# Token products that read their weight columns as pairs from the two halves of the row

## The chip, the core and the metric

The kernel runs on one core of a Trainium2 chip. Its time is the device time of one execution in microseconds (us); lower is better. The core has TensorE (PE in the profile; its weight loads are PEld), VectorE (DVE), ScalarE (ACT), GpSimd (POOL) and SyncE (SP, which issues the DMAs here). SBUF is the working memory with 128 partitions; PSUM holds eight banks of 512 float32 for each partition, into which the matmuls write.

## The reference

It is a decoder trunk with two layers over 256 tokens and 2048 channels, in float32. Layer 0 mixes by causal pooling, layer 1 by attention with dilated windows; each is followed by a gated MLP of width 5504 with a short convolution in time. Two products of layer 1 matter here:

```python
v_shared = (h @ shared_w_v).reshape(B_, S, N_HEADS, HEAD_DIM)
...
def conv_ffn(h, w_up, conv_w, conv_b, w_down):
    u = h @ w_up
    ...
    return (jax.nn.silu(gate) * val) @ w_down
...
ff = conv_ffn(h, ffn_w_up[i], ffn_conv_w[i], ffn_conv_b[i], ffn_w_down[i])
h = layer_norm(DEEPNORM_ALPHA * h + ff, ln2_g[i], ln2_b[i])
```

## The kernel before

Each float32 number is split into a high part `h`, rounded to the type fp32r, and a low part `l`, the rest. A product x w is computed as three: high by high, high by low and low by high. A matmul has a stationary operand of 128 x 128, loaded into TensorE's array, and a moving operand whose columns are streamed through it, up to 512 at a time.

The work is a list of **units**. A unit is a block of a weight matrix, mostly 512 x 512: one DMA of 1 MB brings it to `raw` (`do_load`), ScalarE rounds it to `wh` and VectorE subtracts to get `wl` (`do_split`, L76 and L77), and TensorE uses both. `run_units` goes through the list; loads run up to six units ahead and splits up to three. What follows a product is attached to its last unit (`post`) or put off by some units (`later`).

Most products have the channels as rows of the result: the weights are stationary and the 256 tokens are the moving operand (`mm_quad`, called by `group`; L135 streams 512 columns, high and low part of the tokens as two runs of 256; L136 and L138 to L140 stream 256).

Two families of products have the **tokens as rows** (`group_tm`): there 128 tokens are stationary (`xh`, `xl`), and the weights are moving, 512 columns of `wh` or `wl` at a time. For each of the two halves of the tokens (t = 0, 1) and each block k of 128 input channels there are three matmuls, L162 to L164, that accumulate in the bank `ps[t]`, which the profile calls `t`. These families are

- the values of the attention, `shared_w_v`, four groups of four units, one group after each quarter's keys and queries. `v_post` copies the two banks to `vt`, by ScalarE (L657) and VectorE (L659);
- the down projection of layer 1's MLP, `ffn_w_down[1]`: 43 blocks of 128 input channels by four column groups, in four rounds. `tm_post` adds each finished bank to the residual `HT` (`ht` in the profile) on VectorE (L603). In the last round the layer norm follows: the statistics of each column group (L608), then `finish`, and the output is stored. The last column group does its two token halves one after the other (`apart`).

The order of the instructions on each engine is that of the program text, by units; there is no planner. TensorE's banks come from a pool of eight.

## Time and profile before

| what | value |
|---|---|
| median of 3 runs | 2078.8 us (2077.95 to 2078.83) |
| profiled execution | 2079.46 us |
| its span in the profile | 2077.2 us |
| granted TensorE clock in it | 0.997 of full speed |
| busy: TensorE / VectorE / ScalarE | 99% / 68% / 50% |
| HBM read over the span | 380.01 MB, 184 GB/s read and written |

The span is the time from the first to the last instruction that the profile shows; the execution's time is some 2 us more. "Busy" counts the time in which an engine has at least one instruction under way. A group of the profile is read as line, engine, operation, result <- operands, shapes and count, then total busy time in us and mean duration in ns, then the engine's idle time just before these instructions in us and what ended it. In the profile, "PE 128x512" is a matmul with 512 columns. Numbers of an engine in a window stand as busy us with the count of instructions in brackets. The chain that ended last is followed from the last instruction back to whatever released each step.

### The profile page before, as it was taken

Reading aid. Unit: us, or ns where it says so; the run is one execution under the profiler, and the core shown is the slowest. Engines: PE = TensorE matmul, PEld = TensorE weight load, DVE = VectorE, ACT = ScalarE, POOL = GpSimd, SP = SyncE. Lnnn points to the kernel's source line nnn. Section 1 sums busy time; section 2 is a strip of 40 time slices with the busy share of each in tenths; the row PEclk is TensorE's granted clock in tenths of the full one; section 3 lists DMA queues with packets and bytes.
Section 4 is the critical chain, followed back from the end, with each engine's and each line's share of the span. In section 5 each row is a group of like instructions: output and inputs, shape, how many; then the busy total and the mean of one; then the engine's idle time right before and its main releaser. Section 6 shows DMA issues by size and latency. Waiting matters only on the chain.

```text
span 2077.2 us, 28936 instructions
## 1 busy us (share of the span) xinstructions
PE 2062.0 (99%) x12131; PEld 1819.3 (88%) x12131; DVE 1417.2 (68%) x1765; ACT 1029.2 (50%) x1145; POOL 11.4 (1%) x38
## 2 busy tenths in 40 slices
PE   9999999999999999999999999999999999999997
PEld 9998998888888888889888888999888888888886
DVE  6758787756756766788855667787646664665676
ACT  6545665345534535546644444475535543544553
POOL 2000000000000000000000000000000000000000
PEclk9999999999999999999999999999999999999999
DMA  8655465555555555555555555545555555555453
GB/s 261 214 186 195 148 211 175 202 182 186 180 203 183 183 197 178 178 177 167 199 168 178 162 171 175 197 148 202 184 199 185 183 190 195 183 184 192 162 198 137
DMA packets 195298, 383.99 MB, mean 185 GB/s; under 512 B 7022, under 2 KB 15876, under 8 KB 194912
## 3 DMA queue, kind: packets, MB, share of 16 engines
q1 hardware_dynamic: 194240, 381.71, 53.8%
q8 instruction: 95, 1.56, 0.3%
q0 software_dynamic: 928, 0.44, 0.1%
q14 instruction: 35, 0.29, 0.0%
HBM read 380.01 MB, written 2.10 MB: 184 GB/s over the span
## 4 chain that ended last, share of the span: by engine, by line
PE 98%; DVE 1%; DMA 0%; SPq 0%; issue 0%; ACT 0%; DVEq 0%
PE acc L135 44%; PE acc L136 23%; PE t L162 5%; PE t L164 5%; PE t L163 5%; PE acc L139 5%; PE acc L138 5%; PE acc L140 5%; DVE wl L77 0%; PE s L693 0%; PE o L733 0%; DVE ht L633 0%; PE pT L720 0%; DMA xin<-in_x_dram 0%; PE o L734 0%; PE s L692 0%
## 5 line engine op out<-in xcount | busy, mean ns | idle before, releaser
L77 DVE TENSOR_TENSOR wl<-raw,wh 128x2048 fp32r<-128x2048 f32 (+2 forms) x376 | 821.1, 2187 | 514.8 <-ACT wh L76 504.9
L76 ACT CAST wh<-raw 128x2048 fp32r<-128x2048 f32 (+2 forms) x376 | 685.3, 1828 | 594.3 <-PE acc L135 367.9
L135 PE MATMUL acc<-xc,wh 128*128 128x512 f32 x2752 | 969.1, 396 | 0.0
L136 PE MATMUL acc<-xc,wl 128*128 128x256 f32 x2752 | 772.1, 281 | 0.0
L135 PEld LDWEIGHTS acc<-xc,wh 128*128 128x128 f32 x2752 | 519.1, 189 | 122.2
L136 PEld LDWEIGHTS acc<-xc,wl 128*128 128x128 f32 x2752 | 519.0, 189 | 0.2
L135 PE MATMUL acc<-g,wh 128*128 128x512 f32 x688 | 241.9, 396 | 0.0
L136 PE MATMUL acc<-g,wl 128*128 128x256 f32 x688 | 193.0, 280 | 0.0
L135 PEld LDWEIGHTS acc<-g,wh 128*128 128x128 f32 x688 | 129.9, 189 | 30.6
L518 DVE SCALAR_TENSOR_TENSOR c<-u,cv,c 128x256 f32<-128x256 f32 x344 | 141.9, 478 | 0.7
L162 PE MATMUL t<-wh,g 128*128 128x512 f32 x344 | 136.1, 396 | 0.0
L163 PE MATMUL t<-wl,g 128*128 128x512 f32 x344 | 135.5, 394 | 0.0
L164 PE MATMUL t<-wh,g 128*128 128x512 f32 x344 | 135.4, 394 | 0.0
L136 PEld LDWEIGHTS acc<-g,wl 128*128 128x128 f32 x688 | 130.0, 189 | 0.0
L139 PE MATMUL acc<-xp,wh 128*128 128x258 f32 x384 | 109.2, 284 | 0.0
L138 PE MATMUL acc<-xc,wh 128*128 128x256 f32 x384 | 109.2, 284 | 0.0
L138 PE MATMUL acc<-xp,wh 128*128 128x258 f32 x384 | 109.0, 284 | 0.0
L140 PE MATMUL acc<-xc,wl 128*128 128x256 f32 x384 | 108.8, 283 | 0.0
L139 PE MATMUL acc<-xc,wh 128*128 128x256 f32 x384 | 108.7, 283 | 0.0
L140 PE MATMUL acc<-xp,wl 128*128 128x258 f32 x384 | 107.9, 281 | 0.0
L505 ACT COPY ut<-acc 128x256 f32<-128x256 f32 x140 | 51.6, 371 | 96.3 <-PE acc L136 96.1
L135 PE MATMUL acc<-o,wh 128*128 128x512 f32 x256 | 90.4, 396 | 0.0
(182 smaller groups left out, 2310.8 us busy)
## 6 DMA issues: line engine op xcount, KB each, us to landing
raw<-in_ffn_w_up_dram SPq DMA_DIRECT2D x160, 1024.0 KB, 4.9
raw<-in_ffn_w_down_dram SPq DMA_DIRECT2D x80, 1024.0 KB, 5.0
raw<-in_pool_w_out_dram SPq DMA_DIRECT2D x16, 1024.0 KB, 5.1
raw<-in_shared_w_k_dram SPq DMA_DIRECT2D x16, 1024.0 KB, 5.0
raw<-in_attn_w_q_dram SPq DMA_DIRECT2D x16, 1024.0 KB, 5.1
raw<-in_shared_w_v_dram SPq DMA_DIRECT2D x16, 1024.0 KB, 5.0
raw<-in_attn_w_o_dram SPq DMA_DIRECT2D x16, 1024.0 KB, 5.1
raw<-in_pool_w_in_dram SPq DMA_DIRECT2D x12, 1024.0 KB, 5.3
```

What stands on the lines that cost most here:

```text
L76: A.copy(wh[i][:, s], r[:, s])
L77: V.tensor_tensor(wl[i][:, s], r[:, s], wh[i][:, s].bitcast(F32), OP.subtract)
L135: PE.matmul(ps[m], h[:, k, c], q[:, k, :, :T], start=st, stop=False)
L136: PE.matmul(ps[m][:, :T], l[:, k, c], q[:, k, 0, :T], start=False, stop=sp)
L138: PE.matmul(ps[m][:, :n], h[:, k, c], q[:, k, 0, :n], start=st, stop=False)
L139: PE.matmul(ps[m][:, :n], h[:, k, c], q[:, k, 1, :n], start=False, stop=False)
L140: PE.matmul(ps[m][:, :n], l[:, k, c], q[:, k, 0, :n], start=False, stop=sp)
L162: PE.matmul(ps[t], xh, h[:, k, :], start=j == 0 and k == 0, stop=False)
L163: PE.matmul(ps[t], xh, l[:, k, :], start=False, stop=False)
L164: PE.matmul(ps[t], xl, h[:, k, :], start=False, stop=j == len(r0s) - 1 and k == nk - 1)
L505: A.copy(t, ps[m][:, T:])
L518: V.scalar_tensor_tensor(c[:, m, :], u[:, m, i:i + T], cv[:, i, j:j + 1], c[:, m, :], op0=OP.mult, op1=OP.add)
```

## The change

In `group_tm` the moving operand is read through a view, `twine`: columns 0, 256, 1, 257, 2, 258 and so on, so pairs from the two halves of the 512 columns of a row. The matmul writes its 512 results in a row in the bank, in that order. Where the bank is read, `untwine` takes its words 0, 2, 4 ... as the first half and 1, 3, 5 ... as the second, and `halves2` shows the destination as two halves. The values computed and the places where they end up are those of before. It touches the 1416 matmuls with tokens as rows, the additions to `HT` and the copies to `vt`.

```diff
+    def twine(w):
+        return w.rearrange("p (a c) -> p c a", a=2)
+
+    def untwine(ps):
+        return ps.rearrange("p (c a) -> p a c", a=2)
+
+    def halves2(v):
+        return v.rearrange("p (a c) -> p a c", a=2)
+
     def group_tm(w, r0s, c0, ncol, xqs, post, apart=False):
...
             for k in range(nk):
                 xh, xl = q[:, k, 0, s], q[:, k, 1, s]
-                PE.matmul(ps[t], xh, h[:, k, :], start=j == 0 and k == 0, stop=False)
-                PE.matmul(ps[t], xh, l[:, k, :], start=False, stop=False)
-                PE.matmul(ps[t], xl, h[:, k, :], start=False, stop=j == len(r0s) - 1 and k == nk - 1)
+                hk, lk = twine(h[:, k, :]), twine(l[:, k, :])
+                PE.matmul(ps[t], xh, hk, start=j == 0 and k == 0, stop=False)
+                PE.matmul(ps[t], xh, lk, start=False, stop=False)
+                PE.matmul(ps[t], xl, hk, start=False, stop=j == len(r0s) - 1 and k == nk - 1)
...
         def post(t, ps):
             y = HT[c][:, t, :]
-            V.tensor_tensor(y, y, ps, OP.add)
+            V.tensor_tensor(halves2(y), halves2(y), untwine(ps), OP.add)
...
             if t == 0:
                 vts[c] = pools["attn"].tile([P, 2, 512], F32, name="vt", tag="vt")
-                A.copy(vts[c][:, 0, :], ps)
+                A.copy(halves2(vts[c][:, 0, :]), untwine(ps))
             else:
-                V.tensor_copy(vts[c][:, 1, :], ps)
+                V.tensor_copy(halves2(vts[c][:, 1, :]), untwine(ps))
```

## The prediction

> **What bounds the kernel now.** I read the page's head first, then its slices, then the chain that ended last.

> ```profile
> span 2077.2 us, 28936 instructions
> PE 2062.0 (99%) x12131; PEld 1819.3 (88%) x12131; DVE 1417.2 (68%) x1765; ACT 1029.2 (50%) x1145; POOL 11.4 (1%) x38
> PE   9999999999999999999999999999999999999997
> PEclk9999999999999999999999999999999999999999
> DMA  8655465555555555555555555545555555555453
> PE 98%; DVE 1%; DMA 0%; SPq 0%; issue 0%; ACT 0%; DVEq 0%
> PE acc L135 44%; PE acc L136 23%; PE t L162 5%; PE t L164 5%; PE t L163 5%; PE acc L139 5%; PE acc L138 5%; PE acc L140 5%; DVE wl L77 0%; PE s L693 0%; PE o L733 0%; DVE ht L633 0%; PE pT L720 0%; DMA xin<-in_x_dram 0%; PE o L734 0%; PE s L692 0%
> ```

> TensorE is at work in every slice but the last, at the full granted clock, and 98% of the chain is its matmuls. VectorE has a third of its time free, ScalarE half, the DMA engines about half. So whatever lengthens a matmul lengthens the kernel by as much, and whatever lengthens another engine's work costs nothing until TensorE waits for it. Three entries of the chain, L162 to L164 with 5% each, are the products that the change touches. Next I asked for that tile alone over the whole span, and for its groups.

> ```profile
> core 0: us, PE busy (x) PEld busy (x) DVE busy (x) ACT busy (x), PEclk, DMA share, GB/s
> 0.00:2077.20 2077.20, 333.26 (x1416) 265.55 (x1416) 24.56 (x36) 2.29 (x4) 1.00 0.54 185
> ```

> ```profile
> L162 PE MATMUL t<-wh,g 128*128 128x512 f32 x344 | 136.1, 396 | 0.0
> L162 PEld LDWEIGHTS t<-wh,g 128*128 128x128 f32 x344 | 64.7, 188 | 15.2
> ```

> There are 1416 of these matmuls, and the last column of the group (0.0) says that TensorE does not stand idle before them. A duration of 396 ns is not what one costs, because they overlap. The cost is the distance from one start to the next, which the timeline of TensorE shows: first a stretch of the token products, then one of products with 256 columns.

> ```profile
> 2039.62 0.39 PE L162 MATMUL t<-wh,g 128*128 128x512 f32 x1
> 2039.85 0.39 PE L163 MATMUL t<-wl,g 128*128 128x512 f32 x1
> 2040.08 0.39 PE L164 MATMUL t<-wh,g 128*128 128x512 f32 x1
> ...
> 2061.89 0.39 PE L162 MATMUL t<-wh,g 128*128 128x512 f32 x1
> ```

> ```profile
> 19.83 0.28 PE L139 MATMUL acc<-xc,wh 128*128 128x256 f32 x1
> 19.95 0.28 PE L140 MATMUL acc<-xc,wl 128*128 128x256 f32 x1
> ...
> 21.97 0.28 PE L139 MATMUL acc<-xc,wh 128*128 128x256 f32 x1
> ```

> In the first stretch 96 starts lie between its ends: (2061.89 - 2039.62) / 96 = 0.2320 us for 512 columns. In the second there are 18: (21.97 - 19.83) / 18 = 0.1189 us for 256. The difference over 256 columns is **0.442 ns for a column**, and 5.8 ns are left for each instruction. So a token product is a stream of columns read from SBUF, one after another, with nothing else in it worth counting: 512 x 0.442 = 226.2 of its 232.0 ns. All 1416 take 1416 x 0.2320 = 328.5 us, 15.8% of the span.

> **The change part by part.** *Instructions.* Each engine has the same instructions in the same order as before; none is added, dropped or moved, no DMA and no wait among them. What changes is how three kinds of instruction walk through memory.

> *The matmuls' moving read.* Before, column c follows column c - 1, four bytes on. Now column c of the first half is followed by column c of the second half, 1024 bytes on, then the walk comes back to c + 1. All 512 columns are read and all 512 results written in a row in the bank. The number of columns is the same, so the price is nothing if each still takes 0.442 ns. No matmul of the trace reads its moving operand that way: those of L135 read two runs of 256. So the price has to be bounded. These are the nearest rows, reads of SBUF on the other engines:

> ```profile
> L809 ACT CAST gb<-vec 128x32 fp32r<-128x32 f32 x3 | 0.6, 226 | 0.1
> L76 ACT CAST wh<-raw 128x512 fp32r<-128x512 f32 x16 | 9.0, 628 | 0.4 <-DMA raw<-in_pool_w_in_dram 0.3
> L76 ACT CAST wh<-raw 128x2048 fp32r<-128x2048 f32 x336 | 640.9, 1909 | 560.9 <-PE acc L135 351.7 <-PE t L164 118.0 <-issue 68.6
> ```

> ```profile
> L810 DVE TENSOR_TENSOR gb<-vec,gb 128x32 fp32r<-128x32 f32 x3 | 0.5, 184 | 0.0
> L415 DVE TENSOR_TENSOR edge<-sw,inv 128x28 f32<-128x28 f32 x1 | 0.2, 188 | 0.0
> L415 DVE TENSOR_TENSOR edge<-sw,inv 128x60 f32<-128x60 f32 x1 | 0.2, 221 | 0.1
> L77 DVE TENSOR_TENSOR wl<-raw,wh 128x512 fp32r<-128x512 f32 x16 | 10.1, 680 | 0.2 <-ACT wh L76 0.2
> L77 DVE TENSOR_TENSOR wl<-raw,wh 128x2048 fp32r<-128x2048 f32 x336 | 768.9, 2290 | 488.6 <-ACT wh L76 486.4
> ```

> L809 and L810 read `vec` in just the new manner, as pairs from two places (16 words apart), 32 words in all. On VectorE that took 184 ns, where plain rows took 188 for 28 words and 221 for 60: no extra. On ScalarE 226 ns; its plain casts grow by (1909 - 628) / 1536 = 0.834 ns a word, so 32 plain words would take 628 - 480 x 0.834 = 228: no extra either. That is the **lower end, nothing**. But it binds TensorE weakly. These rows are short, the two places are 64 bytes apart and not 1024, and the engines are slow readers: VectorE takes (2290 - 680) / 1536 = 1.048 ns for a word and TensorE 0.442. A reader that takes a word every 0.442 ns has less than half the time in which a hop could hide.

> For the other end, suppose that the fast stream comes from fetching neighbours together. If each fetch brings two words, a hop wastes one of them and a column takes 2 x 0.442 = 0.884 ns. If a column then took as long as a word on ScalarE it would be 0.834, as on VectorE 1.048. If a fetch brings four and three are wasted, it is 4 x 0.442 = 1.768 ns. Below nothing: the 188 ns of a weight load stand against 232, so at most 44 x 1416 = 62 us could be won. No row suggests that a hop reads faster, and I give that little.

> I take 0.884: it lies between the two rows that show what a word costs a reader that does not get neighbours cheaply, 0.834 and 1.048. That adds 512 x 0.442 = 226.2 ns to each matmul, and 1416 x 226.2 ns = **320.3 us**, all of it on the path, since these matmuls are the chain and idle nowhere. For the range I keep the ends: 0.834 gives 512 x 0.392 = 200.7 ns and 284 us, 1.048 gives 310.3 ns and 439 us, 1.768 gives 678.9 ns and 961 us.

> [...]

> *The reads of the bank.* VectorE's 36 reads of tile `t` and ScalarE's 4 now step by two words in PSUM and write two runs of 256.

> ```profile
> L603 DVE TENSOR_TENSOR ht<-ht,t 128x512 f32<-128x512 f32 x32 | 21.8, 682 | 15.3 <-PE t L164 15.3
> L633 DVE TENSOR_TENSOR ht<-ht,g 128x512 f32<-128x512 f32 x8 | 5.2, 684 | 0.9 <-ACT ht L625 0.9
> ```

> Reading the bank costs no more than reading SBUF now (682 against 684). With step 2 I put the price between nothing and once more the same, 0.68 us; nothing is nearest, as L810 showed for a step. What hides it: VectorE is busy 68% and TensorE waits for none of these (0.0 idle above). Without that cover all of it would be 24.56 + 2.29 = 27 us. Only the last one is on the path:

> ```profile
> 2065.30 0.25 PE t L164
> 2065.55 0.02 issue
> 2065.58 0.70 DVE ht L603
> 2066.28 0.02 issue
> 2066.30 0.70 DVE bn L608
> ```

> That is up to 0.7 us, 0.03%, below what can be told from no change here (I take 0.2%, some 4 us).

> *What is late next.* Where the products of a unit take longer, the loads and splits for the next units gain time; in those stretches nothing but TensorE can be last.

> *Sum.* The profiled execution took 2079.46 us, 2.3 over its span and 0.03% above the median of 2078.8. 2079.5 + 320.3 = **2400 us**; with 0.834 and 1.048 for a column 2364 and 2519, say 2360 to 2520.

> **Rivals.** *The hop is free.* TensorE's read path keeps the two places open at once, so each fetch serves its neighbours later, as the two short rows show on VectorE and ScalarE; or it fetches far enough ahead. The time is then 2079, within 0.2%. For it: L809 and L810. Against it: 0.442 ns a column is more than twice as fast as either. It decides as soon as two alternating streams are held by the reader, and then there is nothing left to lose: the forecast falls to not slower, whatever the distance of the halves.

> *A whole fetch of four words for each column.* Nothing is kept from one column to the next: 1.768 ns, 2079.5 + 961 = 3040 us. [...] For it: TensorE would then be the one reader that gets by far the most from neighbours. Against it: it would be slower for one column than VectorE is for two plain reads and a write of a word (1.048).

> *A part of the hop is hidden.* The read path runs ahead while the 5.8 ns of the instruction and the drain pass, or pays only for the farther half: between 2085 and 2360, at half of the forecast's price 2240.

> *The change doesn't do what it says.* The halves would be read as two runs after all, and nothing would change. The results in the bank would be in another order then, and the reads of the bank undo precisely the order of pairs; I count it within the free case.

> **How the numbers follow.** Two words to a fetch (2360 to 2520): 0.36. Free: 0.32, of which a hundredth or two may fall past 0.2%. Four words, or anything between 2520 and 3045: 0.18. A part hidden (2085 to 2360): 0.09. Beyond 3045: 0.03. Faster by over 0.2%: 0.02. The free case and the dear one are each too likely to be left out, so the range goes from 2075 to 3045; the likeliest alone has 2360 to 2520. Faster 0.02, within 0.2% 0.31, slower 0.67.

> **What the changed profile would show.** The distance between starts of the token products settles all: 0.458 us if I am right, 0.232 if the hop is free, 0.91 if four words are lost. The products with 512 columns at L135, which keep their runs, must hold their pace, and so must the stretch before the first token product. If instead TensorE shows idle time in front of the token products, the loss comes from the banks, and the group of L603 names it. If L603 stays near 682 ns, the step in PSUM is free. The prediction is wrong as a whole if the pace of the token products has not moved.

## The result and the profile after

| | before | after |
|---|---|---|
| median | 2078.57 us (2077.95 to 2078.83, 4 runs) | 2055.38 us (2054.72 to 2055.86, 4 runs) |
| profiled execution | 2079.46 us | 2055.73 us |
| its span | 2077.2 us | 2053.9 us |

The changed kernel is **faster by 1.1%**: ratio 0.9889, 95% interval 0.9871 to 0.9906. The forecast was 2400 us in a range from 2075 to 3045, and a gain had a chance of 0.02. The granted clock was 0.997 in both profiles, so it has no part in the difference. Lines of `group_tm` and below stand ten or so further down now: L162 to L164 are L172 to L174, L603 is L613.

The head of the page of the changed kernel and its chain that ended last read as before:

```profile
span 2053.9 us, 28936 instructions
PE 2038.5 (99%) x12131; PEld 1820.7 (89%) x12131; DVE 1416.9 (69%) x1765; ACT 1029.3 (50%) x1145; POOL 11.4 (1%) x38
PE 98%; DVE 1%; DMA 0%; ACT 0%; issue 0%; SPq 0%; DVEq 0%
```

TensorE is busy for 23.5 us less. The other engines work about as long as before; the weight loads grow by 1.4 us. The tile of the token products alone, over the whole span, and the reads of its bank by VectorE:

```profile
core 0: us, PE busy (x) PEld busy (x) DVE busy (x) ACT busy (x), PEclk, DMA share, GB/s
0.00:2053.90 2053.90, 309.73 (x1416) 267.05 (x1416) 24.50 (x36) 2.28 (x4) 1.00 0.56 187
```

```profile
L613 DVE TENSOR_TENSOR ht<-ht,t 128x512 f32<-128x512 f32 x32 | 21.8, 682 | 8.7 <-PE t L174 8.7
```

333.26 us became 309.73: 23.5 us, which is the whole difference of the spans (23.3). The step of two in PSUM costs VectorE nothing, 682 ns as before. L135, which the change doesn't touch, holds its 396 ns, and the tile `acc` of those products keeps TensorE busy for 1700.9 us as before. TensorE's timeline in the last round shows the new distance from start to start:

```profile
2014.88 0.38 PE L172 MATMUL t<-wh,g 128*128 128x512 f32 x1
...
2041.43 0.38 PE L172 MATMUL t<-wh,g 128*128 128x512 f32 x1
```

There are 123 starts between them: 26.55 / 123 = 0.2159 us, where it was 0.2320. The difference of 16.1 ns by 1416 is 22.8 us. This is none of the three distances that the prediction named as signs (0.458, 0.232, 0.91). A last view shows where the time had been: the same matmuls by tile, as shortest/median/longest duration in ns, first of before, then of after.

```profile
L162 PE MATMUL t<-wh,g x344: 392/394/400, 1477.1 to 2064.7; 128*128 128x512 f32 x172
L164 PE MATMUL t<-wh,g x344: 387/393/403, 1477.6 to 2065.1; 128*128 128x512 f32 x172
```

```profile
L172 PE MATMUL t<-wh,g x344: 378/379/379, 1470.9 to 2041.4; 128*128 128x512 f32 x172
L174 PE MATMUL t<-wh,g x344: 379/379/379, 1471.4 to 2041.9; 128*128 128x512 f32 x172
```

Before, matmuls of one shape took anything from 387 to 403 ns. In these groups they now take 378 or 379. So reading the row straight on had been *losing* time, by a varying amount, and the pairs do not show this loss.

### The profile page after: what moved, and what is told of

Same layout as the page of the kernel before. It is cut to its first block, busy times and chain, and to the rows that moved or that the text cites. A ratio compares the mean times of both kernels' runs of the same rounds, so it can differ in the third digit from the quotient of the medians.

```text
span 2053.9 us, 28936 instructions
## 1 busy us (share of the span) xinstructions
PE 2038.5 (99%) x12131; PEld 1820.7 (89%) x12131; DVE 1416.9 (69%) x1765; ACT 1029.3 (50%) x1145; POOL 11.4 (1%) x38
## 2 busy tenths in 40 slices
PE   9999999999999999999999999999999999999997
## 4 chain that ended last, share of the span: by engine, by line
PE 98%; DVE 1%; DMA 0%; ACT 0%; issue 0%; SPq 0%; DVEq 0%
PE acc L135 45%; PE acc L136 23%; PE t L172 5%; PE t L174 5%; PE t L173 5%; PE acc L139 5%; PE acc L138 5%; PE acc L140 5%; DVE wl L77 0%; DVE ht L643 0%; PE s L703 0%; PE o L743 0%; PE pT L730 0%; DMA xin<-in_x_dram 0%; PE o L744 0%; PE s L702 0%
## 5 line engine op out<-in xcount | busy, mean ns | idle before, releaser
L77 DVE TENSOR_TENSOR wl<-raw,wh 128x2048 fp32r<-128x2048 f32 (+2 forms) x376 | 821.0, 2188 | 499.4 <-ACT wh L76 489.8
L76 ACT CAST wh<-raw 128x2048 fp32r<-128x2048 f32 (+2 forms) x376 | 685.2, 1828 | 576.9 <-PE acc L135 367.8
L135 PE MATMUL acc<-xc,wh 128*128 128x512 f32 x2752 | 969.2, 396 | 0.0
L136 PE MATMUL acc<-xc,wl 128*128 128x256 f32 x2752 | 772.2, 281 | 0.0
L135 PEld LDWEIGHTS acc<-xc,wh 128*128 128x128 f32 x2752 | 519.2, 189 | 122.1
L136 PEld LDWEIGHTS acc<-xc,wl 128*128 128x128 f32 x2752 | 519.0, 189 | 0.2
L135 PE MATMUL acc<-g,wh 128*128 128x512 f32 x688 | 241.9, 396 | 0.0
L136 PE MATMUL acc<-g,wl 128*128 128x256 f32 x688 | 192.9, 280 | 0.0
L135 PEld LDWEIGHTS acc<-g,wh 128*128 128x128 f32 x688 | 129.9, 189 | 30.6
L174 PE MATMUL t<-wh,g 128*128 128x512 f32 x344 | 130.4, 379 | 0.0
L172 PE MATMUL t<-wh,g 128*128 128x512 f32 x344 | 130.4, 379 | 0.0
L173 PE MATMUL t<-wl,g 128*128 128x512 f32 x344 | 130.4, 379 | 0.0
L136 PEld LDWEIGHTS acc<-g,wl 128*128 128x128 f32 x688 | 130.0, 189 | 0.0
L139 PE MATMUL acc<-xp,wh 128*128 128x258 f32 x384 | 109.2, 284 | 0.0
L138 PE MATMUL acc<-xc,wh 128*128 128x256 f32 x384 | 109.1, 284 | 0.0
L138 PE MATMUL acc<-xp,wh 128*128 128x258 f32 x384 | 108.9, 284 | 0.0
L140 PE MATMUL acc<-xc,wl 128*128 128x256 f32 x384 | 108.8, 283 | 0.0
L139 PE MATMUL acc<-xc,wh 128*128 128x256 f32 x384 | 108.6, 283 | 0.0
L140 PE MATMUL acc<-xp,wl 128*128 128x258 f32 x384 | 107.9, 281 | 0.0
L135 PE MATMUL acc<-o,wh 128*128 128x512 f32 x256 | 90.4, 396 | 0.0
```

The lines of the kernel that those rows point to most:

```text
L76: A.copy(wh[i][:, s], r[:, s])
L77: V.tensor_tensor(wl[i][:, s], r[:, s], wh[i][:, s].bitcast(F32), OP.subtract)
L135: PE.matmul(ps[m], h[:, k, c], q[:, k, :, :T], start=st, stop=False)
L136: PE.matmul(ps[m][:, :T], l[:, k, c], q[:, k, 0, :T], start=False, stop=sp)
L138: PE.matmul(ps[m][:, :n], h[:, k, c], q[:, k, 0, :n], start=st, stop=False)
L139: PE.matmul(ps[m][:, :n], h[:, k, c], q[:, k, 1, :n], start=False, stop=False)
```

## The experiments

Four kernels leave out all of the reference's work. They keep weights and tokens in SBUF, begin with small products (`warm`), and then run streams of 48 matmuls in the order of the kernel's products (high by high, high by low, low by high); only the way of reading differs from stream to stream, and each writes a bank with a name of its own. In the profile's groups a stream is one row: its last three numbers are busy us, mean duration in ns and idle time. From start to start is (busy - one duration) / 47; straight rows come to (11.3 - 0.394) / 47 = 0.232 us, the pairs of the change to (10.5 - 0.379) / 47 = 0.215, so the streams show what the kernel does. The first stream of each kernel (`plain`) isn't used: its matmuls took 433 to 458 ns in the mean. Straight rows are run again as `again` or `last`, where they took 394 (403 at the end of b2). Each of these kernels ran once. The loops over the names are written out below.

```python
seq = [(k, a, b) for _ in range(reps) for k in range(4) for a, b in ((0, 0), (0, 1), (1, 0))]
for i, (k, a, b) in enumerate(seq):
    PE.matmul(o, sta(k, a), mov(k, b), start=i == 0, stop=i == len(seq) - 1)
...
run("ways_b", view("p (a c) -> p c a", a=2))
run("near_d", view("p (g a c) -> p g c a", a=2, c=4))
run("run_b", view("p (a c r) -> p c a r", a=2, r=2))
```

### b1: orders of reading

`ways`: columns in turn from 2 (b), 4 (d), 8 (h) or 16 (p) equal parts of the row. `step`: each column 2 (b), 4, 8 or 16 words after the one before. `near`: pairs 2 (b), 4 (d), 8 ... 128 (z) words apart. `run`: runs of 2 (b), 4 (d), 8 ... 64 (y), 128 words from each half in turn.

> The kernel's own work is left out; TensorE only runs streams of 48 float32r matmuls with 512 columns that differ in the order in which the moving row is read. Two theories of the 16 ns that the pairs saved. Theory A (line theory): a row read straight on stalls at each new piece of the row because neighbours come from one place, and any order that keeps two or more far places in turn hides it. Then the plain rows have a mean duration of 394 ns, two, four and eight ways 379, near pairs inside a piece (near_b, near_d) stay at 394, far ones (near_x and on) 379, and runs of two to eight words from both halves 379, growing back to 394 for long runs (run_y, run_z). Theory B (lockstep theory): the straight stream meets the weight load, which is also a straight stream, at the same spot of SBUF again and again; any order that isn't straight breaks the lockstep, so nearly all views, the near pairs too, come to 379 and only plain and the longest runs stay at 394. Rival of both, from the prediction: hops are free only for two places held open; then four and more ways, and steps of 4 words and more (step_d, step_h, step_p), go to 580 ns (0.834 ns a column) or over.

The rows that decide, from the groups of TensorE:

```profile
L75 PE MATMUL again<-w,q 128*128 128x512 f32 x48 | 11.3, 394 | 0.0
L75 PE MATMUL ways_b<-w,q 128*128 128x512 f32 x48 | 10.5, 379 | 0.0
L75 PE MATMUL ways_d<-w,q 128*128 128x512 f32 x48 | 13.5, 445 | 0.0
L75 PE MATMUL ways_h<-w,q 128*128 128x512 f32 x48 | 23.7, 691 | 0.0
L75 PE MATMUL step_b<-w,q 128*128 128x512 f32 x48 | 21.9, 643 | 0.0
L75 PE MATMUL step_h<-w,q 128*128 128x512 f32 x48 | 20.9, 613 | 0.0
L75 PE MATMUL near_b<-w,q 128*128 128x512 f32 x48 | 11.3, 394 | 0.0
L75 PE MATMUL near_d<-w,q 128*128 128x512 f32 x48 | 10.5, 379 | 0.0
L75 PE MATMUL near_z<-w,q 128*128 128x512 f32 x48 | 10.5, 379 | 0.0
L75 PE MATMUL run_b<-w,q 128*128 128x512 f32 x48 | 16.1, 504 | 0.0
L75 PE MATMUL run_d<-w,q 128*128 128x512 f32 x48 | 12.2, 414 | 0.0
L75 PE MATMUL run_y<-w,q 128*128 128x512 f32 x48 | 11.3, 394 | 0.0
```

Neither theory holds. Theory A has four and eight ways and short runs at 379: they are at 445, 691, 504 and 414. Theory B has every order that isn't straight at 379: pairs 2 words apart stay at 394. Pairs 4 words apart are as good as those 256 apart, 379 ns. And the step of 8 words costs (20.9 - 0.613) / 47 = 0.432 us, that of 2 words 0.452: nearly twice the straight row, what the prediction forecast for the change. The rival of both, that hops are free for two places only, fits the steps and eight ways, but it has four ways at 580 ns or over, and they are at 445. Of these orders only pairs come to 379 ns, and not all pairs.

### b2: the weight load, the place, the length, the type

`few_x`: a weight load of 32 columns in place of 128. `stastep`, `stafour`: a load that reads with step 2 or 4. `off_a`: the moving row starts one word later. `tok`: 256 tokens, high and low part, as moving operand (as in L135), `tokhop` the same in pairs 128 tokens apart; `cols_b` 256 columns of weights straight on, `tokhol` 256 tokens in pairs. `bfplain`, `bfhalf`: bfloat16, straight and in pairs.

> The kernel's own work is left out; streams of 48 matmuls as in the run beside it, with other weight loads, places, lengths and types. Theory A (the straight stream stalls by itself): the loss of 15 ns in 394 stays whatever the weight load is: 64 or 32 stationary columns, a load with step 2 or 4, the same load each time. It grows with the columns: 384 columns lose 11, 256 lose 8. Theory B (the straight stream meets the weight load): 64 stationary columns lose half (about 387), 32 a quarter (383), a load with step 2 or 4 changes the loss; shifts of the moving row by 1 to 16 words change it too, which A does not expect beyond a row that starts off a boundary. bfloat16 reads half the bytes: no loss or half under both, 379 to 386. For use: if the token streams of the other products also lose (tok 396), pairs of tokens (tokhop) should take 379 under both.

```profile
L80 PE MATMUL few_x<-w,q 128*32 128x512 f32 x48 | 11.3, 394 | 0.0
L80 PE MATMUL stastep<-w,q 128*128 128x512 f32 x48 | 11.3, 395 | 0.0
L80 PE MATMUL stafour<-w 128*128 128x512 f32 x48 | 11.5, 399 | 0.0
L80 PE MATMUL off_a<-w,q 128*128 128x512 f32 x48 | 11.6, 399 | 0.0
L80 PE MATMUL tok<-q,w 128*128 128x512 f32 x48 | 11.3, 395 | 0.0
L80 PE MATMUL tokhop<-q,w 128*128 128x512 f32 x48 | 10.5, 378 | 0.0
L80 PE MATMUL cols_b<-w,q 128*128 128x256 f32 x48 | 5.9, 282 | 0.0
L80 PE MATMUL tokhol<-q,w 128*128 128x256 f32 x48 | 5.5, 275 | 0.0
L80 PE MATMUL bfplain<-wb,qb 128*128 128x512 bf16 x47 | 10.5, 379 | 0.1
L80 PE MATMUL bfhalf<-wb,qb 128*128 128x512 bf16 x48 | 23.4, 646 | 0.0
L80 PE MATMUL last<-w,q 128*128 128x512 f32 x48 | 11.7, 403 | 0.0
```

The loss does not come from the weight load: with loads of 32 columns in place of 128 the matmuls still take 394 ns, where theory B had 383. Theory B is out. Two of its signs are left open, both small: with a load of step 4, and with a row that starts one word later, the matmuls took 399 ns and with the other loads and starts 393 to 396, but the straight rows at the end of this kernel (`last`) took 403. Why was not tried. In these rows the loss stands with the moving stream of float32r; straight bfloat16 takes 379 ns (the trace lacks one of its 48 records), and for bfloat16 the same pairs are dear, (23.4 - 0.646) / 47 = 0.484 us. Streams of tokens gain from pairs as those of weights do, 378 ns against 395.

### v_only: the pairs in the value products alone

```diff
-                hk, lk = twine(h[:, k, :]), twine(l[:, k, :])
+                hk, lk = (twine(h[:, k, :]), twine(l[:, k, :])) if pairs else (h[:, k, :], l[:, k, :])
...
-        group_tm(shared_w_v, rows4, 512 * hq, 512, xsrcs, v_post(hq))
+        group_tm(shared_w_v, rows4, 512 * hq, 512, xsrcs, v_post(hq), pairs=True)
```

> Pairs in the value products alone (384 of the 1416 matmuls), the down projection as before. If the gain is 16.2 ns for each matmul wherever it stands (start to start 0.216 instead of 0.232 us), the time falls by 384 x 16.2 = 6.2 us to 2072.4, ratio 0.997. If the gain came from elsewhere (order of banks, loads, splits) in the last stage, the ratio is 1.000 here.

The additions to `HT` read their banks straight on again. Measured: 2072.01 us against 2078.86, ratio 0.9968 (0.9956 to 0.9981); by the medians 6.9 us, where 6.2 were expected. In its groups, the value products first, then the down projection:

```profile
L173 PE MATMUL t<-wl,xc 128*128 128x512 f32 x128 | 48.5, 379 | 0.0
...
L173 PE MATMUL t<-wl,g 128*128 128x512 f32 x344 | 135.5, 394 | 0.0
```

The gain goes with the matmuls that read pairs: 379 ns in the value products, 394 in the down projection, as before.

### b3: how far apart, and how much of a piece

`short`: 510 columns straight on. `dist`: pairs 3 (c), 5 (e), 15, 17 (q), 51, 255 (z) words apart. `same`: each of 256 words twice. `use_b`, `use_a`: pairs from the halves that take every second, or every fourth, word and go through the row two or four times.

> The kernel's own work is left out; streams of 48 matmuls. Theory C: the columns are taken two at a time, the first of each two by one reader and the second by another; straight on, both want the same 16-byte piece and get in each other's way, and pairs give each a piece of its own. Then pairs whose places lie 5, 15, 17, 51 or 255 words apart cost 215 ns for 510 columns, though the two cross into their next pieces at different times; 3 apart share a piece part of the time and lie between 215 and 231. Pairs out of two different tiles' rows (apart) 216; the same column twice (same) shares always: 232 or more. Shifts of the pairs by 1, 2 or 3 words change nothing. Each reader using only 2 words (use_b) or 1 (use_a) of a piece before it leaves it: as slow as the eight-way views, 430 to 490. Rival, theory D: a loss of straight rows comes once for each 64 bytes in which the stream has only one place to read from; then 3 apart loses all (231) and 5, 15, 17 lose part, since both places are mostly within one 64-byte piece.

```profile
L75 PE MATMUL short<-w,q 128*128 128x510 f32 x48 | 11.3, 394 | 0.0
L75 PE MATMUL dist_c<-w,q 128*128 128x510 f32 x48 | 13.1, 438 | 0.0
L75 PE MATMUL dist_e<-w,q 128*128 128x510 f32 x48 | 11.9, 409 | 0.0
L75 PE MATMUL dist_q<-w,q 128*128 128x510 f32 x48 | 11.0, 387 | 0.0
L75 PE MATMUL dist_z<-w,q 128*128 128x510 f32 x48 | 10.5, 379 | 0.0
L75 PE MATMUL same<-w,q 128*128 128x512 f32 x48 | 10.5, 379 | 0.0
L75 PE MATMUL use_b<-w,q 128*128 128x512 f32 x48 | 11.3, 394 | 0.0
L75 PE MATMUL use_a<-w,q 128*128 128x512 f32 x48 | 21.9, 632 | 0.0
```

### b4: theory E with numbers given beforehand

> The kernel's own work is left out; streams of 48 matmuls. Theory E, formed on the two streams before: the columns go in turn to two readers (odd and even columns of the stream), each fetches the row in pieces of 4 words, and what counts is how many columns a reader takes from a piece before it needs the next: 4 or more cost nothing (216 ns for 512 columns), 2 cost 16 ns (232), 1 costs twice the time and more (430 to 460). So: each word twice (two_a) 216, every second word twice (two_b) 232, every fourth word twice, 256 columns (two_d), 215 to 230 where 256 straight columns take 119; each word four times (four_a) 216, every second one four times (four_b) 216, every fourth four times (four_d) 232; pairs 4 words apart in groups of 8 (line) 216, the same from a start 4 words on (swap) 216, but from a start 2 words on (half) 232, since each reader then has its four words in two pieces. Every third word in pairs from the halves (use_c) uses 2, 1 and 1 of three pieces: some 340. Rival, theory F: it is enough that the two columns of a pair come from different places (or are the same), the pieces don't matter: then half 216, four_d 216 and two_b 216.

```profile
L75 PE MATMUL two_b<-w,q 128*128 128x512 f32 x48 | 11.3, 394 | 0.0
L75 PE MATMUL two_d<-w,q 128*128 128x256 f32 x48 | 11.2, 408 | 0.0
L75 PE MATMUL four_b<-w,q 128*128 128x512 f32 x48 | 10.5, 379 | 0.0
L75 PE MATMUL four_d<-w,q 128*128 128x512 f32 x48 | 11.3, 394 | 0.0
L75 PE MATMUL swap<-w,q 128*128 128x512 f32 x48 | 10.5, 379 | 0.0
L75 PE MATMUL half<-w,q 128*128 128x512 f32 x48 | 11.2, 391 | 0.0
L75 PE MATMUL use_c<-w,q 128*128 128x510 f32 x48 | 16.5, 518 | 0.0
```

`two_a`, `four_a` and `line` are at 379 ns too. All come out as theory E has them, to within 3 ns: `two_b` 0.232 us, `four_b` 0.215, `four_d` 0.232, `two_d` (11.2 - 0.408) / 47 = 0.230, `use_c` (16.5 - 0.518) / 47 = 0.340. `swap` and `half` are the sharpest: the same pairs, moved by 4 words, 0.215; moved by 2, which by the count puts each reader's four words in two pieces, 0.230. Theory F, for which the pieces don't matter, is out.

### near4 and near2: theory E in the kernel

```diff
-        return w.rearrange("p (a c) -> p c a", a=2)
+        return w.rearrange("p (g a c) -> p g c a", a=2, c=4)
```

with the views of the bank and the destination to match; near2 has c=2.

> As the change, but the pairs lie 4 words apart, in groups of 8 columns: 0, 4, 1, 5, 2, 6, 3, 7, 8, 12, ... Theory E: as good as the halves of the row, 2055.4 us, ratio 0.989. If the distance of the halves is what counts, 2078.7.

> As the change, but the pairs lie 2 words apart, in groups of 4 columns: 0, 2, 1, 3, 4, 6, 5, 7, ... Each column hops as in the change. Theory E: each reader still gets 2 words of a piece, as in straight rows, so nothing is won: 2078.7 us, ratio 1.000. If pairs as such helped, 2055.4.

Pairs 4 words apart: 2055.66 us against 2078.83, ratio 0.9891 (0.9875 to 0.9908), as the change. Pairs 2 words apart: 2078.93, ratio 1.000 (0.9991 to 1.0009), no gain at all, though both hop at every column and read the bank with the same kind of view. One group of each, near4 first:

```profile
L172 PE MATMUL t<-wh,g 128*128 128x512 f32 x344 | 130.4, 379 | 0.0
```

```profile
L172 PE MATMUL t<-wh,g 128*128 128x512 f32 x344 | 136.1, 396 | 0.0
```

So in the kernel, too, neither the size of the hop nor the pairs as such decide; the count of theory E tells the two apart, 379 ns from 396.

### quarters and steps8: the forecast's price in the kernel

```diff
-        return w.rearrange("p (a c) -> p c a", a=2)
+        return w.rearrange("p (a c) -> p c a", a=4)
```

with the other two views to match; steps8 has a=64.

> As the change, with four ways in place of two: columns 0, 128, 256, 384, 1, ... By the stream measured alone (278 ns from start to start) the 1416 token products cost 46 ns more than straight rows: 2079 + 65 = 2144 us. If the prediction's rival were right that a hop is free in the kernel, 2055 or 2079.

> As the change, with 64 ways: each column lies 8 words behind the one before, and the row is gone through eight times. By the stream measured alone (431 ns) the token products cost 199.5 ns more than straight rows: 2079 + 282 = 2361 us. That would be the price that the prediction forecast for the pairs (a hop at each column, 0.83 to 0.88 ns a column: 2364 to 2400).

One execution each: 2145.41 us for four ways (expected 2144) and 2360.0 us for steps of 8 words (expected 2361). One group of their token products, first of four ways, then of steps of 8 words:

```profile
L172 PE MATMUL t<-wh,g 128*128 128x512 f32 x344 | 153.8, 447 | 0.0
```

```profile
L172 PE MATMUL t<-wh,g 128*128 128x512 f32 x344 | 210.8, 613 | 0.0
```

The streams measured alone (0.278 and 0.432 us) carry over to the kernel, to within 1.5 us of its time. So nothing hid a slower stream there; the loss went straight to the end, as the prediction had it.

### full: pairs in all products

The tokens as moving operand are read in pairs t, t + 128 as well, and all banks of these products are read with a step of two. For the 258 columns of mode "x", the row of `xp` holds each half of the tokens with one of the two extra columns behind it.

```diff
-                    PE.matmul(ps[m], h[:, k, c], q[:, k, :, :T], start=st, stop=False)
-                    PE.matmul(ps[m][:, :T], l[:, k, c], q[:, k, 0, :T], start=False, stop=sp)
+                    PE.matmul(ps[m], h[:, k, c], twine_hl(q[:, k, :, :T]), start=st, stop=False)
+                    PE.matmul(ps[m][:, :T], l[:, k, c], twine(q[:, k, 0, :T]), start=False, stop=sp)
...
-                    V.tensor_tensor(y, y, ps[m][:, :T], OP.add)
+                    V.tensor_tensor(halves2(y), halves2(y), untwine(ps[m][:, :T]), OP.add)
```

> Pairs in all products, with the token products as in the change; where the tokens are the moving operand, pairs of token t and t + 128, and the banks read with a step of 2. If the gain belongs to the order of reading and not to the token products, 3952 matmuls with 512 columns come from 0.2336 to 0.2159 us (70 us), 3952 with 256 columns from 0.1181 to 0.1116 (26 us), some 2500 with 256 or 258 columns from 0.120 to 0.1116 (21 us): 2055.4 - 117 = 1938 us. Rival: VectorE and ScalarE, which read banks ten times as often here with a step of 2, or the splits become the bound, since TensorE runs 6% faster: then TensorE shows idle time in front of its matmuls and the time stays between 1960 and 2055.

Measured: **1947.12 us** (1946.59 to 1948.06, 4 runs) against 2078.67, ratio 0.9368 (0.9353 to 0.9384), 6.3% faster than before and 5.3% faster than the change (1947.12 / 2055.38). Its page, and groups of the products with tokens as moving operand (L153 and L154 are L135 and L136 of before, L157 is L138):

```profile
PE 1927.6 (99%) x12131; PEld 1781.3 (92%) x12131; DVE 1414.6 (73%) x1765; ACT 1026.6 (53%) x1157; POOL 11.4 (1%) x38
L153 PE MATMUL acc<-xc,wh 128*128 128x512 f32 x2752 | 903.6, 382 | 0.0
L154 PE MATMUL acc<-xc,wl 128*128 128x256 f32 x2752 | 750.1, 273 | 0.0
L157 PE MATMUL acc<-xp,wh 128*128 128x258 f32 x384 | 106.9, 278 | 0.0
L157 PE MATMUL acc<-xc,wh 128*128 128x256 f32 x384 | 106.9, 278 | 0.0
```

The rival did not come: VectorE and ScalarE work as long as before (1414.6 and 1026.6 us) and TensorE does not wait in front of these products (0.0). The time lies 9 us above the expected 1938. L153 comes to 382 ns and not 379, but L154 behind it comes to 273 and not the 275 of `tokhol`; the products with 256 or 258 columns from `xc` and `xp` come to 277 or 278. All products of the tile `acc` keep TensorE busy for 1589.35 us, where the changed kernel had 1700.91: they won 111.6 us of the 117 expected. Why not all, and where the last 3 us of that are, was not tried.

## Why the prediction was wrong, point by point

- **What bounds the kernel**: right. The token products' change reached the end: 23.5 us of busy time came to 23.3 of span, and four and 64 ways to 2145.41 and 2360.0 us where their streams alone gave 2144 and 2361.
- **The instructions, the bank reads, what is late next**: right. L613 takes 682 ns as L603 did, and TensorE does not wait in front of the token products (0.0).
- **The moving read** is the step that failed, in two premises. The first was "if each fetch brings two words, a hop wastes one of them", priced at 0.884 ns a column and +320.3 us. The runs show a price of that kind, but for orders that theory E counts as one column to a piece: steps of 8 words gave 2360.0 us, in the forecast's own range of 2360 to 2520. The pairs show no such price: their distance is 0.2159 us. No run shows how many words a fetch brings. The second premise was that 0.442 ns a column is what a straight stream costs when nothing is wrong. It contained a loss: 16.1 of 232.0 ns. The term was +226.2 ns for a matmul and measured -16.1.
- **The sign of the evidence**: L809 and L810 read pairs in the same manner and lost nothing (226 ns where plain casts came to 228, and 184 where plain rows took 188 for 28 words and 221 for 60). They were set aside because those engines read slowly. That let two rows on the very access give way to rows (0.834, 1.048) on a word's price in straight reading.
- **Below nothing**: the bound of 62 us, from the 188 ns of a weight load, held the measured 23.2 by luck. It is no bound: the loads overlap too, and in the stretch that the prediction shows, L139 and L140 start 0.1189 us apart while a load of L139 takes 190 ns in the mean. A gain got a chance of 0.02 since "no row suggests that a hop reads faster". One view did suggest that something was to be had: the spread of 387 to 403 ns among matmuls of one shape. After the change it is 378 to 379. The prediction read means only. That a row without spread loses nothing was not shown.
- **The rivals**: that the hop is free came nearest, at 2079 us, but it, too, saw nothing to be won. Its mechanism (two places held open) is not shown by any trace; that pairs 2 words apart take 0.232 us and four ways 0.278 shows that a hop is not free whatever the order.

## What to carry to other kernels

A float32r moving operand read straight on took 7% longer here than one read in pairs (0.232 against 0.216 us for 512 columns). Orders that gave 0.215 us were pairs from the two halves of the row and pairs 4 words apart that start with the row (`near_d`) or 4 words on (`swap`); the same pairs from 2 words on took 0.230 (`half`). The order is undone where the bank is read, which cost nothing here (L613, 682 ns as before). Do not carry it to bfloat16 (646 ns in pairs, 379 straight) nor to four ways (0.278) or steps (0.432 to 0.461). And before a row's mean is taken for a floor, look at its shortest and longest: a spread among equal instructions can go with a loss that some other order does not have, as 387 to 403 ns here against 378 to 379.

## What the runs showed of the hardware

Theory E counts columns per reader and piece and met the numbers given beforehand, but the two readers and the pieces are a picture; the traces show times alone. It does not explain all: four ways (0.278 us) and runs of 2 (0.332) are cheaper than the 0.432 to 0.490 of other orders with one column to a piece, and runs of 4 (0.251), of 8 and 16 (0.242 and 0.240) are dearer than the 0.232 of two. A straight start on an odd word (`off_a`) took (11.6 - 0.399) / 47 = 0.238, but the straight rows at the end of the same kernel took (11.7 - 0.403) / 47 = 0.240. Why bfloat16 in pairs takes 0.484 us is open as well, and writing the bank in the row's order, which would spare the views where it is read, was not tried.
